# Front transfers ordered by first use, modulation weights in contiguous rows, a deeper ring of x tiles, a new simulation of transfers in the scheduler

## The chip, the cores and the metric

The kernel runs on all 8 cores of one Trainium2 chip, one batch element on each core. The metric is the device time of the slowest core in microseconds (us). A program on all cores has a second, slower state in some executions (one die at a lower clock). Engines: PE (TensorE, matmul), DVE (VectorE), ACT (ScalarE), POOL (GpSimd, which also issues the casting DMAs of weights) and SP (which issues the other DMAs).

## The reference

One decoder layer with conditioning. In outline:

```python
mod = silu(c) @ w_ada + b_ada                    # six modulation vectors of 1024; w_ada is 1024 x 6144 float32
sh1, sc1, g1, sh2, sc2, g2 = split(mod, 6)
h = rmsnorm(x, norm_mix_g) * (1 + sc1) + sh1     # x: 2048 x 1024 on each core
proj = h @ w_in                                  # 1440 columns: q and kv latents, rope key, window q, k, v
y = concat(mla_group(...), swa_group(...))       # causal latent attention, sliding-window attention
x = x + g1 * (y @ w_o)
h = rmsnorm(x, norm_mlp_g) * (1 + sc2) + sh2
x = x + g2 * (relu(h @ w_up) ** 2 @ w_down)
return rmsnorm(x, final_g)
```

## The kernel before

The tokens are worked on in four groups (0 to 3) of four x tiles (128 rows each). The "front" is what must come before steady matmul work: the first x tiles, the modulation weights (`wada`, 24 loads of 1 MB of float32, written as bf16), the input projection (`winl` for latents, `winr` for the rest), `wkvk`/`wkvv`, the rope table `csq` and the window mask `em` (1 MB).

The program lists operations with what they read and write. A list scheduler inside it simulates the engines and the DMA queues and so fixes one static order of instructions for each engine before anything runs. Each engine then works strictly in that order. The parts that matter:

```python
# --- scheduler: how long a transfer takes in its simulation (before)
if o.dma:
    free[e] = t + o.dur
    oth = "sp" if e == "pool" else "pool"
    s_ = max(chan[e], t + o.dur)
    nb = max(0.0, chan[oth] - s_) / lastpk[oth] if lastpk[oth] else 0.0
    nc_ = min(o.npk, nb)
    chan[e] = s_ + o.npk * o.pk + nc_ * lastpk[oth]
    chan[oth] += nc_ * o.pk        # but transfers already placed keep their old end
    lastpk[e] = o.pk
    o.end = chan[e] + 2000.0

# --- dependences: a later writer of a buffer waits for its earlier readers ("war")
for b in w:
    self._add_dep(op, b.w, "waw")
    for x in b.r:
        self._add_dep(op, x, "war")
# ... cut ...
NXT = 2                                              # ring of x tiles
XT, bXT = ring("XT", NXT, [128, D], F32, "SA")
# ... cut ...
# modulation weights lie over memory that attention uses later: K (rows of 256 elements,
# as K is [128, 8, 2048]) or V (contiguous)
for g in range(1, NG):
    for half in range(2):
        c0 = g * 512 + half * 256
        wada_over(f"K{g}{'ab'[half]}", a_Kg[g], K_[:, :, c0:c0 + 256])
    wada_over(f"V{g}", a_V[g], ...)                  # 4096 bytes in a row
WADA_SLOT = {4: "K1a", 5: "K1b", 6: "V1", 7: "K2a", 0: "K2b", 1: "V2", 2: "K3a", 3: "K3b", 12: "V3", 13: "K1a", 14: "K1b",
             15: "V1", 16: "K2a", 17: "K2b", 18: "V2", 19: "K3a", 8: "K3b", 9: "V3", ...}
# ... cut ...
for c in range(4):
    wada_load(4 + c)                                 # POOL queue, in this order
    win_lat(c)
for c in range(4):
    wada_load(c)
# wkvk, wkvv, winr[0], winr[1], then loads 12, 13, 14, 15, wqb, 16, ...
load_cs(0, [bWKVV])     # csq waits for wkvv to land, by being listed as a reader of it
# ... cut ...
# later: wkvv is scaled in place by DVE; as a writer of wkvv it waits for csq
S.op("dve", lambda h: h.tensor_scalar(out=WKVV[:, c, :], in0=WKVV[:, c, :], scalar1=GKVA[:, c:c + 1],
                                      scalar2=None, op0=ALU.mult), r=[bWKVV, bPAR], w=[bWKVV])
S.dma("sp", lambda h: h.dma_start(out=EM, in_=em_d), bEM, w=[bEM])
```

The softmax here doesn't subtract the row's maximum and nothing guards it: scores larger than these inputs give would overflow.

Of the kernel before, what the change touches and what calls it, by code (L numbers as in the profile page):

```python
# [86 lines left out]

class Engine:


    def __init__(self, h):
        self.h = h

    def __getattr__(self, name):
        f = getattr(self.h, name)
        return lambda *a, **k: f(*[settle_arg(x) for x in a], **{n: settle_arg(x) for n, x in k.items()})  # L96

# [29 lines left out]
class Sched:  # L127
# [115 lines left out]
    def schedule(self):  # L243
# [5 lines left out]
        for t in tenants.values():  # L249
            if t.eager:  # L250
                continue
            mine = {id(o) for o in t.ops}
            for o in t.ops[1:]:
                for (d, dv, kind) in list(o.deps):
                    if id(d) not in mine and any(set(u.allowed) & set(t.allowed) for u in d.tens):
                        t.ops[0].deps.append((d, 0, "order"))
# [12 lines left out]
        free = {e: 0.0 for e in self.ENGS}  # L269
        chan = {"pool": 0.0, "sp": 0.0}  # L270
        lastpk = {"pool": 0.0, "sp": 0.0}
        order = {e: [] for e in self.ENGS}
# [21 lines left out]
        def place(o, t):  # L294
# [27 lines left out]
            return t  # L322

        last_in = [None] * 8
        for o in self.all:
# [3 lines left out]
        while left:  # L329
            best = None  # L330
            for e in self.ENGS:
                if now[e]:
                    t = free[e]
                elif fut[e]:
                    t = max(free[e], fut[e][0][0])
                else:
                    continue
                if best is None or t < best[0]:
                    best = (t, e)
            if best is None:  # L340
                raise RuntimeError(f"no bank for {[(o.idx, o.fn.__code__.co_firstlineno) for o in parked]}")
# [15 lines left out]
            if o.dma:  # L357

                free[e] = t + o.dur
                oth = "sp" if e == "pool" else "pool"  # L360
                s_ = max(chan[e], t + o.dur)
                nb = max(0.0, chan[oth] - s_) / lastpk[oth] if lastpk[oth] else 0.0
                nc_ = min(o.npk, nb)
                chan[e] = s_ + o.npk * o.pk + nc_ * lastpk[oth]
                chan[oth] += nc_ * o.pk
                lastpk[e] = o.pk
                o.end = chan[e] + 2000.0
            else:
                o.end = t + o.dur + (165.0 if e == "pe" else 0.0)
                free[e] = max(t + 20.0, o.end - self.OVER[e] ) if e != "pe" else t + o.dur  # L370
            order[e].append(o)
            left -= 1
            for tn in o.tens:
                tn.left -= 1
                if tn.left == 0:
# [4 lines left out]
                    for w in back:  # L380
                        heapq.heappush(fut[w.eng], (max(w.rdy, min(bank_at[tn.i:tn.i + tn.width])), w.pri, w.idx))
            for j in succ[i_]:
                npred[j] -= 1
                if npred[j] == 0:
                    release(self.all[j])
        self.ops = order
        self.makespan = max(o.end for o in self.all)

    def emit(self, nc, es, block, handles):
        def newsem(name):  # L390
            return es.enter_context(nc.semaphore(name))
# [29 lines left out]
        def run(e, h):  # L421
            seen = {}
            hh = Engine(h)
            for o in self.ops[e]:
                need = {}
                for (d, dv, kind) in o.deps:
                    if skip(o, d, kind):
                        continue
                    if d.dma:
                        k, v = d.dbuf.dsem, dv  # L430
                    else:
                        k, v = esem[d.eng], d.cnt
                    kk = k.num
                    if seen.get(kk, 0) >= v:
                        continue
                    if kk not in need or need[kk][1] < v:
                        need[kk] = (k, v)
                for kk, (k, v) in need.items():
                    h.wait_ge(k, v)  # L439
                    seen[kk] = v  # L440
                ins = o.fn(hh)
                if o.dma:
                    ins.then_inc(o.dbuf.dsem, 16)
                elif o.sig:
                    ins.then_inc(esem[e], 1)
# [79 lines left out]
def build_program():  # L525
# [29 lines left out]
    with es:  # L555
# [9 lines left out]
        def bk(t, rows=None, cols=None):  # L565
            r0, r1 = rows if rows else (0, 128)
            c0, c1 = cols if cols else (0, 512)
            return Lazy(lambda: PS[r0:r1, t.i or 0, c0:c1])

        def bk_bf(t):  # L570
            return Lazy(lambda: PS[:, t.i or 0, :].bitcast(BF16))

        def bk_pair(t):
            return Lazy(lambda: PS[:, t.i or 0:(t.i or 0) + 2, :])

# [143 lines left out]

        for g in range(1, NG):  # L720
            for half in range(2):
                c0 = g * 512 + half * 256
                wada_over(f"K{g}{'ab'[half]}", a_Kg[g], K_[:, :, c0:c0 + 256])
            wada_over(f"V{g}", a_V[g], AR.ap(Alloc("", a_V[g].lo, a_V[g].lo + 4096, ""), [128, 8, 256], BF16))
        for i in range(4):
            WADA[f"B{i}"], bWADA[f"B{i}"] = one(f"WADAB{i}", [128, 8, 256], BF16, "B")
        WADA_SLOT = {4: "K1a", 5: "K1b", 6: "V1", 7: "K2a", 0: "K2b", 1: "V2", 2: "K3a", 3: "K3b", 12: "V3", 13: "K1a", 14: "K1b",
                     15: "V1", 16: "K2a", 17: "K2b", 18: "V2", 19: "K3a", 8: "K3b", 9: "V3", 10: "V3", 11: "V3",
                     20: "B0", 21: "B1", 22: "B2", 23: "B3"}
# [61 lines left out]
        def load_x(t, after=()):  # L791
            s_ = t % NXT
            S.dma("sp", lambda h: h.dma_start(out=XT[s_], in_=x_d[t * 128:(t + 1) * 128, :]), bXT[s_], r=after,
                  w=[bXT[s_]])

        for t in range(NXT):
            load_x(t)
# [78 lines left out]
        def a_norm(G):  # L876
            st = nxt_of("sta", 4)
            for j in range(4):
                t = 4 * G + j
                if t >= NXT:  # L880
                    load_x(t, [[], [bWINL[2]], [bWINR[0]], [bWINR[1]]][G])
                sumsq(XT[t % NXT], bXT[t % NXT], st, j, XN[t % 4], bXN[t % 4])
                rstd4(st, j, 1, D)
                S.op("dve", lambda h, t=t, j=j: h.tensor_scalar(out=XN[t % 4], in0=XT[t % NXT], scalar1=STA[st][:, 8 + j:9 + j],
                                                               scalar2=None, op0=ALU.mult),
                     r=[bXT[t % NXT], bSTA[st]], w=[bXN[t % 4]])

# [188 lines left out]
        S.dma("pool", lambda h: h.dma_start(out=WQB.rearrange("p a b -> p (a b)"), in_=wqb_d), bWQB, w=[bWQB])  # L1076
        for n2 in (16, 17, 18, 19, 8):
            wada_load(n2)
# [18 lines left out]
        for n2 in (12, 13, 14, 15):  # L1097
            ada_step(n2)
        wada_load(9)
        a_rope(1)  # L1100
# [37 lines left out]
        SWA_SCALE = 0.125  # L1138
        S.dma("sp", lambda h: h.dma_start(out=EM, in_=em_d), bEM, w=[bEM])

# [10 lines left out]
        def score(t):  # L1151
            return Lazy(lambda: PS.rearrange("p a b -> p (a b)")[:, 512 * (t.i or 0):512 * ((t.i or 0) + t.width)])

# [521 lines left out]
```

## Time and profile before

| | before |
|---|---|
| time, 40 runs: median (lowest) | 913.6 us (910.8) |
| profiled run, slowest core | 912.8 us |
| PE busy | 807.3 us, 88% |
| 512 B weight packets in the first 130 us (packet records) | 12288 |
| wkvv lands / csq of group 0 lands | 60.2 / 73.8 us |

The page of the kernel before: busy time, then the span in 40 slices of 22.8 us (tenths of busy time; PEclk is the granted PE clock; DMA is the mean busy share of 16 engines), then DMA packets by size.

```profile
span 912.8 us, 15934 instructions; the slowest of 8 cores (897.4 to 912.8 us)
...
PE 807.3 (88%) x5578; PEld 408.2 (45%) x5578; DVE 390.8 (43%) x677; ACT 408.6 (45%) x662; POOL 199.2 (22%) x164
...
PE   0536989989989897867989999999999999999996
...
PEclk9967899999999999979989999999999999999999
DMA  9999972164032548967482004140223511002113
...
DMA packets 47469, 101.47 MB, mean 111 GB/s; under 512 B 3488, under 2 KB 24096, under 8 KB 47264
```

In the first three slices PE is mostly idle while the DMA row is full. The sixteenth to nineteenth slice (342 to 433 us) are a second thin place: the output projection, overlapped with attention's end.

The chain of waits of the kernel before, two pieces of it (start us, length, what):

```profile
10.75 49.40 DMA arena<-wkvv
60.22 13.61 DMA arena<-csq
74.65 0.76 DVE arena L96
75.55 3.16 PE ps L96 x22
...
368.84 14.80 DMA x1s<-arena
383.76 9.13 DMA arena<-x
```

The front ends when wkvv has landed, then csq. In the second thin place the chain is a store of an x1 tile, then the load of an x tile behind it. All the kernel's own instructions carry line 96 in this trace, because of a helper.

Waits of the kernel before in the first 130 us (engine waiting, what for, us in total, times, longest):

```profile
PE ps L96 <- DMA arena<-wada: 15.5, 2, 15.0
DVE arena L96 <- DMA arena<-csq: 13.7, 1, 13.7
```

Busy time by stretches (us from the start: PE, PE loads, DVE, ACT, POOL; granted clock, DMA share, GB/s as written):

```profile
core 5: us, PE busy (x) PEld busy (x) DVE busy (x) ACT busy (x) POOL busy (x), PEclk, DMA share, GB/s
60.00:75.00 15.00, 3.17 (x9) 0.71 (x9) 1.13 (x4) 5.75 (x13) 0.00 (x0) 0.50 0.98 153
85.00:115.00 30.00, 29.79 (x255) 16.23 (x253) 15.14 (x27) 12.63 (x25) 0.76 (x1) 0.91 1.11 207
370.00:400.00 30.00, 18.66 (x159) 9.45 (x157) 8.73 (x14) 14.19 (x26) 2.29 (x2) 0.88 0.93 262
```

PE does 3.2 us of work between 60 and 75 us and is full from 85 to 115. The clock of 0.50 in the empty stretch is what the Trainium skill ("TensorE: Matmul & The Clock Gate", Part 1) describes, a half clock after an idle window of about 3.4 us. This trace agrees: its half-clock records last 3.4 us or multiples of it (the one that the end cuts off aside). At half clock PE also works at half pace: matmuls of 512 columns follow each other every 427 ns in these records and every 216 ns at full clock. So an idle gap can cost a little more than its length.

### The profile page before, as it was taken

How to read it: one execution, taken by the hardware profiler on the slowest of the kernel's cores; microseconds unless marked ns; L12 is line 12 of the kernel's file. 1: busy time of each engine (PE TensorE's matmuls, PEld its weight loads, DVE VectorE, ACT ScalarE, POOL GpSimd, SP SyncE). 2: the span in 40 equal slices, each digit the busy share in tenths (PEclk: the TensorE clock that was granted, in tenths of full speed). 3: DMA queues.
4: the chain of work that ended last, by engine and by line, in shares of the span. 5: the costliest groups of instructions: out<-in, count | busy, mean ns of one | idle time of the engine just before them, and what ended most of it. 6: DMA issues, size and time to landing. Idle time of an engine off the chain costs nothing.

```text
span 912.8 us, 15934 instructions; the slowest of 8 cores (897.4 to 912.8 us)
## 1 busy us (share of the span) xinstructions
PE 807.3 (88%) x5578; PEld 408.2 (45%) x5578; DVE 390.8 (43%) x677; ACT 408.6 (45%) x662; POOL 199.2 (22%) x164
## 2 busy tenths in 40 slices
PE   0536989989989897867989999999999999999996
PEld 0323545655546454434444444444444444444442
DVE  1325477465253448335646112441115533325546
ACT  2244376686888685535200443224442224224334
POOL 6010065265369552100034000000000000111120
PEclk9967899999999999979989999999999999999999
DMA  9999972164032548967482004140223511002113
GB/s 190 200 177 179 226 139 66 53 111 113 35 64 56 172 142 237 228 219 232 169 199 78 1 8 86 48 138 1 41 52 93 184 60 57 24 1 92 69 65 144
DMA packets 47469, 101.47 MB, mean 111 GB/s; under 512 B 3488, under 2 KB 24096, under 8 KB 47264
## 3 DMA queue, kind: packets, MB, share of 16 engines
q1 hardware_dynamic: 28432, 73.06, 25.1%
q0 software_dynamic: 18960, 27.40, 19.3%
q8 instruction: 47, 0.77, 0.3%
q14 instruction: 30, 0.25, 0.1%
HBM read 104.77 MB, written 20.97 MB: 138 GB/s over the span
## 4 chain that ended last, share of the span: by engine, by line
PE 78%; DMA 11%; ACT 3%; DVE 3%; issue 3%; POOL 2%; SPq 0%; DVEq 0%; ACTq 0%; POOLq 0%
PE ps L96 78%; DMA arena<-wkvv 5%; DVE arena L96 3%; ACT arena L96 3%; POOL arena L96 2%; DMA x1s<-arena 2%; DMA arena<-csq 1%; DMA arena<-wdn 1%; DMA arena<-x 1%; DMA mxs<-arena 1%; ACT ps L96 0%; SPq L96 0%; DVEq L439 0%; ACTq L439 0%; SPq L439 0%
## 5 line engine op out<-in xcount | busy, mean ns | idle before, releaser
L96 PE MATMUL ps<-arena 128*128 128x512 bf16 (+4 forms) x5578 | 807.3, 305 | 96.5 <-DVE arena L96 63.6
L96 PEld LDWEIGHTS ps<-arena 128*128 128x128 bf16 x5578 | 408.2, 99 | 495.1 <-issue 162.3
L96 ACT ACTIVATE arena<-ps 128x1024 bf16<-128x1024 f32 (+4 forms) x319 | 243.9, 787 | 330.7 <-PE ps L96 328.0
L96 DVE TENSOR_TENSOR arena<-ps,arena 128x512 f32<-128x512 f32 (+5 forms) x292 | 152.2, 535 | 257.4 <-PE ps L96 243.8
L96 POOL TENSOR_TENSOR arena<-arena 128x512 bf16<-128x512 bf16 (+3 forms) x103 | 162.8, 1593 | 420.7 <-DVE arena L96 246.7
L96 ACT ACTIVATE arena<-arena 128x512 bf16<-128x512 f32 (+3 forms) x264 | 149.0, 570 | 153.8 <-DVE arena L96 74.3
L96 DVE TENSOR_TENSOR arena<-arena 128x1024 bf16<-128x1024 f32 (+4 forms) x51 | 63.8, 1255 | 31.8 <-DMA arena<-wdn 28.9
L96 DVE COPY arena<-ps 128x512 f32<-128x512 f32 (+2 forms) x64 | 41.2, 656 | 71.6 <-PE ps L96 65.4
L96 DVE TENSOR_SCALAR arena<-arena 128x1024 bf16<-128x1024 f32 (+3 forms) x40 | 30.1, 754 | 54.6 <-ACT arena L96 38.0
L96 POOL DMA_DIRECT2D arena<-wup x16 | 8.7, 555 | 175.5 <-PE ps L96 175.5
L96 DVE TENSOR_SCALAR arena<-ps,arena 128x512 bf16<-128x512 bf16 (+1 forms) x72 | 34.9, 533 | 18.1 <-PE ps L96 17.7
L96 DVE TENSOR_SCALAR arena<-ps 128x512 f32<-128x512 f32 x32 | 21.7, 688 | 43.3 <-PE ps L96 39.2
L96 POOL DMA_DIRECT2D arena<-wada x24 | 18.7, 782 | 77.8 <-PE ps L96 76.1
L96 DVE SCALAR_TENSOR_TENSOR arena<-arena 128x1024 f32<-128x1024 f32 (+1 forms) x23 | 21.3, 926 | 9.7 <-ACT arena L96 9.1
L96 DVE SCALAR_TENSOR_TENSOR arena<-arena,ps 128x512 bf16<-128x512 f32 x20 | 13.7, 741 | 4.0 <-ACT ps L96 2.7
L96 ACT ACTIVATE arena<-ps,arena 128x512 bf16<-128x512 f32 x12 | 8.3, 688 | 12.0 <-PE ps L96 12.0
L96 DVE RECIPROCAL arena<-ps 128x4 f32<-128x4 f32 x32 | 5.6, 176 | 17.5 <-PE ps L96 17.4
L96 DVE CAST arena<-ps 128x512 bf16<-128x512 f32 x16 | 10.4, 687 | 2.2 <-PE ps L96 2.2
L96 ACT ACTIVATION_READ_ACCUMULATOR arena<-arena 128x1 f32 x49 | 9.2, 189 | 0.0
L96 ACT ACTIVATE ps<-ps,arena 128x512 f32<-128x512 f32 x8 | 5.2, 662 | 0.8 <-PE ps L96 0.8
L96 POOL DMA_DIRECT2D arena<-wo x8 | 4.4, 559 | 4.7 <-PE ps L96 4.7
L96 ACT ACTIVATE ps<-ps 128x512 f32<-128x512 f32 x8 | 4.5, 595 | 0.2
(14 smaller groups left out, 16.0 us busy)
## 6 DMA issues: line engine op xcount, KB each, us to landing
arena<-x SPq DMA_DIRECT2D x32, 512.0 KB, 8.0
arena<-wdn SPq DMA_DIRECT2D x32, 512.0 KB, 4.1
arena<-wada POOLq DMA_DIRECT2D x24, 512.0 KB, 37.3
arena<-wup POOLq DMA_DIRECT2D x16, 512.0 KB, 10.0
out<-arena SPq DMA_DIRECT2D x15, 512.0 KB, 2.6
x1s<-arena SPq DMA_DIRECT2D x12, 512.0 KB, 5.2
arena<-x1s SPq DMA_DIRECT2D x12, 512.0 KB, 3.2
mxs<-arena SPq DMA_DIRECT2D x12, 256.0 KB, 3.6
```

Of the source, the lines that this page charges most:

```text
L96: return lambda *a, **k: f(*[settle_arg(x) for x in a], **{n: settle_arg(x) for n, x in k.items()})
```

## The change

The intent is to bring bytes in the order in which they are first needed, in longer rows, with more x tiles under way. Five parts, cut to their core (the scheduler deals out eight banks, parts of the memory that matmuls write to):

```diff
@@ memory: slots of the modulation weights
-        for g in range(1, NG):
+        for g in (2, 3):
             for half in range(2):
                 wada_over(f"K{g}{'ab'[half]}", ...)      # rows of 256 elements
+        # contiguous slots of 4096 B over V, window q, mix, PE32, em and QG buffers
-        WADA_SLOT = {4: "K1a", 5: "K1b", 6: "V1", 7: "K2a", 0: "K2b", 1: "V2", 2: "K3a", 3: "K3b", 12: "V3", 13: "K1a", 14: "K1b",
-                     15: "V1", 16: "K2a", 17: "K2b", 18: "V2", 19: "K3a", 8: "K3b", 9: "V3", ...
+        WADA_SLOT = {4: "V1", 5: "V2", 6: "V3", 7: "SWQ0", 0: "SWQ1", 1: "PE32", 2: "EM", 3: "MIX0", 12: "MIX1", 13: "QG", 14: "V1",
+                     15: "PE32", 16: "V2", 17: "V3", 18: "K2a", 9: "K2b", 19: "K3a", 8: "K3b", ...
@@ x tiles: five slots for groups 0 and 1, four loads at once
+        XTS = [0, 1, 2, 3, 0, 1, 4, 3] + [0, 1] * 4
-        for t in range(NXT):
+        for t in range(4):
             load_x(t)
@@ em after w_in, load 9 earlier
-        S.dma("sp", lambda h: h.dma_start(out=EM, in_=em_d), bEM, w=[bEM])
+        S.dma("sp", lambda h: h.dma_start(out=EM, in_=em_d), bEM, r=[bWINR[1]], w=[bEM])
@@ scheduler: the simulation of transfers
-                chan[e] = s_ + o.npk * o.pk + nc_ * lastpk[oth]
-                chan[oth] += nc_ * o.pk
-                o.end = chan[e] + 2000.0
+                dma_run(t)                     # both queues advance together, a packet of each in turn;
+                queue[e].append([o, o.npk])    # a transfer ends only when its packets have gone
@@ scheduler: banks
-                    if id(d) not in mine and any(set(u.allowed) & set(t.allowed) for u in d.tens):
+                    if id(d) not in mine and d.tens and (d.eng == "pe" or any(set(u.allowed) & set(t.allowed) for u in d.tens)):
```

The rest of the diff makes the program build faster and gives instructions their own line numbers. It does not touch csq's false reader.

More of the change, by code (lines that the diff above doesn't have):

```diff
@@ L86, in settle_arg, with lazy, settle_views @@
     return v.get() if type(v) is Lazy else v
-class Engine:
-    def __init__(self, h):
-        self.h = h
-    def __getattr__(self, name):
-        f = getattr(self.h, name)
-        return lambda *a, **k: f(*[settle_arg(x) for x in a], **{n: settle_arg(x) for n, x in k.items()})
+EMITTING = [False]
+def lazy(fn):
+    return fn() if EMITTING[0] else Lazy(fn)
+def settle_views(f):
+    for c in f.__closure__ or ():
+        if type(c.cell_contents) is Lazy:
+            c.cell_contents = c.cell_contents.get()
+    if f.__defaults__:
+        f.__defaults__ = tuple(settle_arg(v) for v in f.__defaults__)
 class Op:
@@ L269, in schedule @@
         free = {e: 0.0 for e in self.ENGS}
-        chan = {"pool": 0.0, "sp": 0.0}
-        lastpk = {"pool": 0.0, "sp": 0.0}
+        queue = {"pool": [], "sp": []}
+        dma_t = [0.0]
         order = {e: [] for e in self.ENGS}
@@ L322, in place, with dma_next, dma_run, done @@
             return t
+        def dma_next():
+            a, b = queue["pool"], queue["sp"]
+            if a and b:
+                n = min(a[0][1], b[0][1])
+                return dma_t[0] + n * (a[0][0].pk + b[0][0].pk), n
+            if a or b:
+                q = (a or b)[0]
+                return dma_t[0] + q[1] * q[0].pk, q[1]
+            return None
+        def dma_run(to):
+            a, b = queue["pool"], queue["sp"]
+            if to > dma_t[0] and (a or b):
+                n = (to - dma_t[0]) / sum(q[0][0].pk for q in (a, b) if q)
+                for q in (a, b):
+                    if q:
+                        q[0][1] -= n
+            dma_t[0] = max(dma_t[0], to)
+        def done(o):
+            for j in succ[o.idx]:
+                npred[j] -= 1
+                if npred[j] == 0:
+                    release(self.all[j])
         last_in = [None] * 8
@@ L339, in schedule @@
                     best = (t, e)
+            nd = dma_next()
+            if nd is not None and (best is None or nd[0] <= best[0]):
+                dma_run(nd[0])
+                for q in queue.values():
+                    if q and q[0][1] <= 1e-6:
+                        d = q.pop(0)[0]
+                        d.end = nd[0] + 2000.0
+                        done(d)
+                continue
             if best is None:
@@ L359, in schedule @@
                 free[e] = t + o.dur
-                oth = "sp" if e == "pool" else "pool"
-                s_ = max(chan[e], t + o.dur)
-                nb = max(0.0, chan[oth] - s_) / lastpk[oth] if lastpk[oth] else 0.0
-                nc_ = min(o.npk, nb)
-                chan[e] = s_ + o.npk * o.pk + nc_ * lastpk[oth]
-                chan[oth] += nc_ * o.pk
-                lastpk[e] = o.pk
-                o.end = chan[e] + 2000.0
+                dma_run(t)
+                queue[e].append([o, o.npk])
             else:
@@ L381, in schedule @@
                         heapq.heappush(fut[w.eng], (max(w.rdy, min(bank_at[tn.i:tn.i + tn.width])), w.pri, w.idx))
-            for j in succ[i_]:
-                npred[j] -= 1
-                if npred[j] == 0:
-                    release(self.all[j])
+            if not o.dma:
+                done(o)
         self.ops = order
@@ L389, in emit @@
     def emit(self, nc, es, block, handles):
+        EMITTING[0] = True
         def newsem(name):
@@ L422, in run @@
             seen = {}
-            hh = Engine(h)
             for o in self.ops[e]:
@@ L440, in run @@
                     seen[kk] = v
-                ins = o.fn(hh)
+                settle_views(o.fn)
+                ins = o.fn(h)
                 if o.dma:
@@ L567, in bk @@
             c0, c1 = cols if cols else (0, 512)
-            return Lazy(lambda: PS[r0:r1, t.i or 0, c0:c1])
+            return lazy(lambda: PS[r0:r1, t.i or 0, c0:c1])
         def bk_bf(t):
-            return Lazy(lambda: PS[:, t.i or 0, :].bitcast(BF16))
+            return lazy(lambda: PS[:, t.i or 0, :].bitcast(BF16))
         def bk_pair(t):
-            return Lazy(lambda: PS[:, t.i or 0:(t.i or 0) + 2, :])
+            return lazy(lambda: PS[:, t.i or 0:(t.i or 0) + 2, :])
         def take_bank(allowed, width=1):
@@ L718, in wada_over, with over, wada_one @@
             bWADA[name] = Buf(a2.name, a2)
-        for g in range(1, NG):
+        def over(name, bases, nbytes):
+            a2 = Alloc(name, bases[0].lo, bases[0].lo + nbytes, "SA")
+            assert all(b.lo == a.hi for a, b in zip(bases, bases[1:])) and bases[-1].hi >= a2.hi
+            for b in bases:
+                a2.overl.append(b)
+                b.overl.append(a2)
+            return a2
+        def wada_one(name, bases):
+            a2 = over("WADA" + name, bases, 4096)
+            WADA[name], bWADA[name] = AR.ap(a2, [128, 8, 256], BF16), Buf(a2.name, a2)
+        for g in (2, 3):
             for half in range(2):
@@ L723, in build_program @@
                 wada_over(f"K{g}{'ab'[half]}", a_Kg[g], K_[:, :, c0:c0 + 256])
-            wada_over(f"V{g}", a_V[g], AR.ap(Alloc("", a_V[g].lo, a_V[g].lo + 4096, ""), [128, 8, 256], BF16))
+        for g in range(1, NG):
+            wada_one(f"V{g}", [a_V[g]])
+        for i in range(2):
+            wada_one(f"SWQ{i}", [bSWQ_[i].alloc])
+            wada_one(f"MIX{i}", [bMIX[2 * i].alloc, bMIX[2 * i + 1].alloc])
+        wada_one("PE32", [bPE32[0].alloc])
+        wada_one("EM", [bEM.alloc])
+        wada_one("QG", [b.alloc for b in bQG[0:4]])
+        xt_over = [over("XT2", [bH1T[1][0].alloc], 4096), over("XT3", [b.alloc for b in bPT[0:2]], 4096),
+                   over("XT4", [b.alloc for b in bPTS[0:2]], 4096)]
+        for a2 in xt_over:
+            XT.append(AR.ap(a2, [128, D], F32))
+            bXT.append(Buf(a2.name, a2))
+        XTS = [0, 1, 2, 3, 0, 1, 4, 3] + [0, 1] * 4
         for i in range(4):
             WADA[f"B{i}"], bWADA[f"B{i}"] = one(f"WADAB{i}", [128, 8, 256], BF16, "B")
-        WADA_SLOT = {4: "K1a", 5: "K1b", 6: "V1", 7: "K2a", 0: "K2b", 1: "V2", 2: "K3a", 3: "K3b", 12: "V3", 13: "K1a", 14: "K1b",
-                     15: "V1", 16: "K2a", 17: "K2b", 18: "V2", 19: "K3a", 8: "K3b", 9: "V3", 10: "V3", 11: "V3",
+        WADA_SLOT = {4: "V1", 5: "V2", 6: "V3", 7: "SWQ0", 0: "SWQ1", 1: "PE32", 2: "EM", 3: "MIX0", 12: "MIX1", 13: "QG", 14: "V1",
+                     15: "PE32", 16: "V2", 17: "V3", 18: "K2a", 9: "K2b", 19: "K3a", 8: "K3b", 10: "V3", 11: "V3",
                      20: "B0", 21: "B1", 22: "B2", 23: "B3"}
@@ L791, in load_x @@
         def load_x(t, after=()):
-            s_ = t % NXT
+            s_ = XTS[t]
             S.dma("sp", lambda h: h.dma_start(out=XT[s_], in_=x_d[t * 128:(t + 1) * 128, :]), bXT[s_], r=after,
                   w=[bXT[s_]])
-        for t in range(NXT):
+        for t in range(4):
             load_x(t)
@@ L879, in a_norm @@
                 t = 4 * G + j
-                if t >= NXT:
+                if t >= 4:
                     load_x(t, [[], [bWINL[2]], [bWINR[0]], [bWINR[1]]][G])
-                sumsq(XT[t % NXT], bXT[t % NXT], st, j, XN[t % 4], bXN[t % 4])
+                sumsq(XT[XTS[t]], bXT[XTS[t]], st, j, XN[t % 4], bXN[t % 4])
                 rstd4(st, j, 1, D)
-                S.op("dve", lambda h, t=t, j=j: h.tensor_scalar(out=XN[t % 4], in0=XT[t % NXT], scalar1=STA[st][:, 8 + j:9 + j],
+                S.op("dve", lambda h, t=t, j=j: h.tensor_scalar(out=XN[t % 4], in0=XT[XTS[t]], scalar1=STA[st][:, 8 + j:9 + j],
                                                                scalar2=None, op0=ALU.mult),
-                     r=[bXT[t % NXT], bSTA[st]], w=[bXN[t % 4]])
+                     r=[bXT[XTS[t]], bSTA[st]], w=[bXN[t % 4]])
         def a_tr(G, kp):
@@ L1076, in build_program @@
         S.dma("pool", lambda h: h.dma_start(out=WQB.rearrange("p a b -> p (a b)"), in_=wqb_d), bWQB, w=[bWQB])
-        for n2 in (16, 17, 18, 19, 8):
+        for n2 in (16, 17, 18, 9, 19, 8):
             wada_load(n2)
@@ L1098, in build_program @@
             ada_step(n2)
-        wada_load(9)
         a_rope(1)
@@ L1151, in score @@
         def score(t):
-            return Lazy(lambda: PS.rearrange("p a b -> p (a b)")[:, 512 * (t.i or 0):512 * ((t.i or 0) + t.width)])
+            return lazy(lambda: PS.rearrange("p a b -> p (a b)")[:, 512 * (t.i or 0):512 * ((t.i or 0) + t.width)])
         class MlaUnit:
```

## The prediction

> **What bounds the kernel now.** TensorE is busy for 88% of the span (the page), but not in the front. By stretches, PE works 23.5 us of the first 75, 8.5 of 75–85, 29.8 of 85–115, 17.3 of 115–135, then over 90%. The DMA engines are busy all through 5–130 us (the page's DMA row). Counting float32 source bytes (weights are cast to bf16 on the way), about 17.5 MB arrive by 60 us, some 300 GB/s. The Trainium skill ("HBM Reference", Specifications) gives 358 GB/s per core when both of a pair stream; the trace runs at about 85% of that. So the front is limited by bytes and their order.
>
> The chain of waits: wkvv landing from 10.8 to 60.2 us, then the csq table until 73.8 (13.6 us for 256 KB, sharing the engines with w_in's 6.6 KB packets of 0.7–0.8 us), then DVE, then PE at 75.5. VectorE stands 13.7 us on csq because csq is issued after wkvv as its "reader", and scaling wkvv must wait for that reader. Behind it stands the normalization of x tile 7, so the group-1 transposes wait too.
>
> **What the change does.**
> 1. em (1 MB) moves from 2.4 us to after w_in: 1.05/0.3 = 3.5 us less DMA ahead of wkvv.
> 2. Twelve modulation loads had 1024 packets of 512 B (mean 67 ns: 4.3 us of 16 engines each); now most have 128 of 4 KB (324–400 ns: 2.6–3.2 us). But elapsed throughput differs less: stretches of nearly only 512 B packets move 300–310 source GB/s, those with 4 KB packets 320–330. Six such loads ahead of wkvv save perhaps 1–3 us, not 7.
> 3. Four x tiles go out at once; x2, x3 were issued at 17 us or later, x6, x7 up to 49 us. Latents of group 0 can run near 33 us instead of 42–47, and group 1's transposes (3.8 us of PE, 3.4 of DVE) can fill the wait for wkvv.
> 4. Some weight slots no longer wait for an earlier load's use. The scheduler's DMA model also changes, so instructions elsewhere are reordered; an uncosted shift of a few us either way.
>
> **Critical path.** wkvv lands near 54–56 us instead of 60. csq behind it still takes 10–13 us: nothing removes that false wait. VectorE goes on at about 67–69; PE's steady run starts 5–7 us earlier with up to 4 us of transposes done: 5–11 us in all. Some is given back, because bytes up to 130 us are the same: em, bada, csq and x8–x11 now crowd 65–90 us, and wqb (landed 94.1, DVE waited 2.1 us) may come only 4 us earlier, a longer wait there. After 135 us PE should merely shift.
>
> Prediction 904 us, 8 in 10 between 892 and 912. Faster by over 2% (below 895): 0.17; within 2%: 0.81; slower: 0.02.
>
> **What would show it.** (a) em lands after w_in; (b) packets of 512 B in the first 130 us fall from 12288 to about a third; (c) wkvv lands near 55; (d) VectorE still waits 8–13 us on csq; (e) group-0 latents by 37 us, group-1 transposes before csq; (f) PE's dense run starts near 66–70 rather than 75.5; (g) PE busy stays near 807 us; (h) PE idle outside the front unchanged within 4 us.
>
> **What would make it wrong.** Throughput of 4 KB rows far above 330 GB/s, or the new order freeing DVE from csq: 890–895. A new DVE stall on wqb, or PE on late modulation weights: 910 or more. Or the reordering changes attention and the output stage (DMA waits of 5–15 us near 300, 370–392 and 422 us).

## The result

| | before | after |
|---|---|---|
| median (lowest) | 913.6 us (910.8), 40 runs | 902.3 us (899.3), 20 runs |
| ratio of fast runs | | 0.9889, 95% interval 0.9874 to 0.9904 |
| PE busy, profiled core | 807.3 us | 808.4 us |
| 512 B weight packets in the first 130 us | 12288 | 4096 |
| wkvv / csq land | 60.2 / 73.8 us | 54.8 / 67.6 us |

A ratio here is the mean time of one kernel's fast runs over that of the other's in the same rounds, so it is not quite the ratio of the quoted medians.

The page of the kernel after, the lines that answer to those of before:

```profile
span 902.4 us, 15926 instructions; the slowest of 8 cores (887.2 to 902.4 us)
...
PE 808.4 (90%) x5578; PEld 409.4 (45%) x5578; DVE 387.9 (43%) x677; ACT 407.3 (45%) x662; POOL 198.9 (22%) x164
...
PE   0659699999999897898788999999999999999996
...
PEclk9959799999999997999899999999999999999998
DMA  9999952075042549968471022220313411002113
...
DMA packets 40301, 101.47 MB, mean 112 GB/s; under 512 B 3488, under 2 KB 15904, under 8 KB 40096
```

The bytes are the same, the packets 7168 fewer. PE is fuller in the second to fourth slice and thinner in the fifth (90 to 113 us). Next, the chain of waits of the kernel after:

```profile
8.53 46.28 DMA arena<-wkvv
54.88 12.70 DMA arena<-csq
...
67.95 0.75 DVE arena L1004
68.84 1.69 PE ps L842 x7
...
365.64 11.55 DMA x1s<-arena
377.32 4.34 DMA arena<-x
```

wkvv lands 5.4 us earlier and csq still follows it. The waits of the kernel after in its first 130 us:

```profile
PE ps L842 <- DMA arena<-wada: 17.9, 2, 11.2
...
DVE arena L1096 <- DMA arena<-csq: 2.6, 1, 2.6
```

DVE now waits 2.6 us for csq instead of 13.7: the order puts the norms and the evacuation of group 1's transposes ahead of scaling wkvv. The stretches of the kernel after:

```profile
core 0: us, PE busy (x) PEld busy (x) DVE busy (x) ACT busy (x) POOL busy (x), PEclk, DMA share, GB/s
60.00:75.00 15.00, 11.54 (x46) 4.20 (x47) 8.10 (x15) 10.78 (x18) 0.00 (x0) 0.85 1.00 203
85.00:115.00 30.00, 21.05 (x166) 12.19 (x165) 15.94 (x32) 9.76 (x22) 0.00 (x0) 0.83 1.16 237
370.00:400.00 30.00, 25.75 (x242) 14.49 (x240) 12.54 (x26) 18.00 (x28) 2.30 (x2) 0.94 0.83 267
```

There are three movements: more PE work early, less between 85 and 115 us, more between 370 and 400 us. The bare windows mix them, because the two kernels are at different points of their work. So the rest of this text uses **milestones: the time at which PE has done 25, 40, 60 ... us of its work, taken from the trace's matmul records of one profiled run, mean of the eight cores**. The standard deviation between cores is 1 to 3.4 us at 60 us of work and 2 to 9 us late, so the mean of eight is known to about 1 us early and 1 to 3 late. Differences in microseconds from before are in brackets.

| PE work done, us | 25 | 40 | 60 | 100 | 300 | 330 | 430 |
|---|---|---|---|---|---|---|---|
| before | 76.3 | 92.2 | 112.4 | 156.3 | 371.1 | 412.1 | 522.2 |
| after | 63.7 (-12.6) | 80.0 (-12.2) | 104.2 (-8.2) | 148.2 (-8.1) | 365.7 (-5.4) | 400.9 (-11.3) | 512.0 (-10.2) |

The front gains 12.6 us. By 60 us of work 4.4 are given back, and by 300 another 2.8 (no more than its error). The output stage (300 to 330) then gains 5.9.

A caution, which the comparisons below need: PE time at half clock is counted here like any other, though it does half the work, so a kernel whose front runs at a lower clock reaches an early milestone too soon. The trace's clock records allow a correction, each microsecond of PE work weighted with the granted clock; a table of it stands under e10. The correction leaves most of after's gain (11.2 us at 25), but not that of some of the runs below.

What happens there shows in the chain's two DMA pieces above: together 23.9 us in before and 15.9 in after. The SP queue's timelines, before and then after (start us, length, what):

```profile
381.54 0.61 SPq L96 DMA_DIRECT2D arena<-h2s  x1
...
383.76 8.43 SPq L96 DMA_DIRECT2D arena<-x  x3
```

```profile
377.32 0.33 SPq L1381 DMA_DIRECT2D arena<-x  x1
...
378.91 0.87 SPq L1453 DMA_DIRECT2D arena<-h2s  x1
```

Before, the x tile that the chain needs was issued behind a 1 MB load of h2, which only the MLP needs; after, ahead of it. PE's timeline of before, and the chain's stretch in before and in after:

```profile
393.82 0.59 PE L96 MATMUL ps<-arena 128*128 128x512 bf16 x1 [7.60 <-DVE arena L96]
...
368.84:392.89 24.05, 15.93 (x146) 8.50 (x143) 7.40 (x12) 13.25 (x23) 2.29 (x2) 0.93 1.01 272
```

```profile
365.64:381.66 16.02, 14.63 (x140) 8.19 (x138) 6.79 (x11) 12.30 (x22) 2.09 (x2) 1.00 0.96 278
```

PE stood 7.6 us at the end of that chain in before and was busy for 15.9 of its 24.0 us. In after it is busy for 14.6 of 16.0 us and goes on soon after. No line of the change's data parts touches these transfers: the scheduler's order does. That the place of the h2 load alone is the reason was not isolated.

### The profile page after: what moved, and what is told of

Same layout as the page of the kernel before. It is cut to its first block, busy times and chain, and to the rows that moved or that the text cites. A ratio compares the mean times of both kernels' runs of the same rounds, so it can differ in the third digit from the quotient of the medians.

```text
span 902.4 us, 15926 instructions; the slowest of 8 cores (887.2 to 902.4 us)
## 1 busy us (share of the span) xinstructions
PE 808.4 (90%) x5578; PEld 409.4 (45%) x5578; DVE 387.9 (43%) x677; ACT 407.3 (45%) x662; POOL 198.9 (22%) x164
## 4 chain that ended last, share of the span: by engine, by line
PE 76%; DMA 16%; DVE 3%; ACT 2%; issue 2%; POOL 1%; SPq 0%; DVEq 0%; ACTq 0%; POOLq 0%
PE ps L842 63%; PE ps L1225 6%; DMA arena<-wkvv 5%; DMA arena<-wdn 3%; PE ps L1249 3%; DMA arena<-arena 2%; DMA arena<-csq 1%; DMA x1s<-arena 1%; PE ps L1272 1%; DMA arena<-h2s 1%; PE ps L1297 1%; PE ps L1334 1%; DMA mxs<-arena 1%; PE ps L1414 1%; DVE arena L1449 1%
## 5 line engine op out<-in xcount | busy, mean ns | idle before, releaser
L842 PE MATMUL ps<-arena 128*128 128x512 bf16 (+3 forms) x3380 | 684.7, 353 | 37.2 <-DMA arena<-wada 17.9
L1476 ACT ACTIVATE arena<-ps 128x512 f32<-128x512 f32 x96 | 57.3, 597 | 261.4 <-PE ps L842 261.3
L1233 ACT ACTIVATE arena<-ps 128x1024 bf16<-128x1024 f32 (+1 forms) x160 | 138.3, 896 | 56.5 <-PE ps L1249 35.3
L1614 DVE TENSOR_TENSOR arena<-ps,arena 128x512 f32<-128x512 f32 x104 | 70.8, 689 | 148.7 <-PE ps L842 148.1
L928 ACT ACTIVATE arena<-arena 128x1024 bf16<-128x1024 f32 x47 | 49.6, 1056 | 117.4 <-DVE arena L1614 35.6
L1225 PE MATMUL ps<-arena 128*128 128x512 bf16 (+3 forms) x416 | 88.6, 309 | 4.2 <-ACT arena L1233 3.0
L1279 POOL TENSOR_TENSOR arena<-arena 128x1024 bf16<-128x1024 f32 x31 | 74.4, 2399 | 42.2 <-PE ps L1249 17.6
L1238 POOL TENSOR_TENSOR arena<-arena 128x512 bf16<-128x512 bf16 x32 | 39.2, 1226 | 153.0 <-ACT arena L1233 152.8
L1249 PE MATMUL ps<-arena 128*128 128x65 bf16 x1088 | 65.4, 195 | 2.6 <-ACT arena L1233 1.1
L1478 ACT ACTIVATE arena<-arena 128x512 bf16<-128x512 f32 x96 | 60.4, 629 | 8.7
L1449 DVE TENSOR_TENSOR arena<-arena 128x1024 bf16<-128x1024 f32 x32 | 41.6, 1306 | 37.6 <-DMA arena<-wdn 37.5
L1388 DVE TENSOR_TENSOR arena<-ps,arena 128x512 f32<-128x512 f32 x32 | 22.0, 686 | 26.3 <-PE ps L842 16.2
## 6 DMA issues: line engine op xcount, KB each, us to landing
arena<-x SPq DMA_DIRECT2D x32, 512.0 KB, 9.5
arena<-wdn SPq DMA_DIRECT2D x32, 512.0 KB, 4.3
arena<-wada POOLq DMA_DIRECT2D x24, 512.0 KB, 38.6
arena<-wup POOLq DMA_DIRECT2D x16, 512.0 KB, 9.5
out<-arena SPq DMA_DIRECT2D x15, 512.0 KB, 2.6
x1s<-arena SPq DMA_DIRECT2D x12, 512.0 KB, 5.8
arena<-x1s SPq DMA_DIRECT2D x12, 512.0 KB, 3.2
```

Of the source, the lines that this page charges most:

```text
L842: S.op("pe", lambda h, i=i: h.matmul(out, lhsT=lhs_list[i], rhs=rhs_list[i], start=(i == 0), stop=(i == n - 1)), r=rbufs[i], w=[bankb[bank]])
L928: S.op("act", lambda h: h.activation(out=dst, in_=src, func=AF.Square, accum_out=STA[st][:, j:j + 1]), r=[bsrc], w=[bSTA[st], bdst])
L1225: S.op("pe", lambda h, c=c, j=j, q0=q0, n=n: h.matmul(score(t)[:, c:c + n], lhsT=K_[:, hh, j * 128:(j + 1) * 128], rhs=QG[q][:, q0:q0 + n] ...
L1233: S.op("act", lambda h: h.activation(out=PT[p][:, 0:n], in_=score(t)[:, 0:n], func=AF.Exp, scale=MLA_SCALE), r=[t.buf], w=[bPT[p]])
L1238: S.op("pool", lambda h: h.tensor_tensor(out=v, in0=v, in1=TRI.unsqueeze(1).to_broadcast([128, m, 128]), op=ALU.mult), r=[bPT[p], bTRI], w ...
L1249: sp=(self.last and i == len(blocks) - 1): h.matmul(bk(ob, None, (qb * 65, qb * 65 + 65)), lhsT=PT[p][:, c:c + 128], rhs=vaug(j, hh), star ...
```

## The experiments

Theory F: the front gains from its data (fewer bytes ahead of wkvv, longer rows, more x tiles at once). Theory O: the order of instructions, from a better simulation of transfers, makes the gain. All ratios are of fast runs, against the kernel before in the same rounds; a time in us beside them is the median of all runs, slow ones included. The kernel after was measured at 0.9889 in its own rounds.

### 1. Two by two: data and order

**e1**: the kernel before with the scheduler's new function, nothing else.

```diff
-    def schedule(self):  # of before
+    def schedule(self):  # of after
```

> The kernel before with only the scheduler's new transfer model and bank rule, no buffer, slot or em change. Theory F (the front gains because fewer bytes and longer rows come ahead of wkvv and more x tiles go out at once): the landing of wkvv stays near 60 us, the PE milestones of the front (time at which 25 us of PE work are done, mean of the eight cores: 76.3 before, 63.7 after) stay within 3 us of before, and the time is 910 to 915. Theory O (the new order of instructions makes the gain): the milestone falls by more than 6 us and the time is 902 to 907.

Measured: 909.1 us, ratio 0.9933 (0.9916 to 0.9951). Milestones: 25 at 67.6 (-8.8), 60 at 106.0 (-6.3), 300 at 368.4 (-2.6), 330 at 403.8 (-8.4). wkvv landed at 61.5. So F alone is wrong: with every byte where it was, the order is worth 6 us, a little less than O expected.

The new function holds two changes, the simulation of transfers and the rule for banks, and no run separates them. The orders themselves can be compared without a chip: built with the bank rule alone, the kernel before keeps its order on every engine up to PE's 666th matmul (126 to 135 us in the trace of before). So what the order does in the front comes from the simulation. Further on both move instructions, and how the rest divides is not shown.

**e2**: the kernel after with the scheduling function of before.

```diff
-    def schedule(self):  # of after
+    def schedule(self):  # of before
```

> The kernel after with the scheduling function of before (old transfer model and bank rule), all data changes kept. F: wkvv lands at 54 to 56 us, the 25 us milestone stays within 3 us of after's 63.7, time 901 to 906. O: the milestone goes back by more than 6 us, time 909 to 915. The part of the gain that comes after 300 us of PE work (5.5 us in the profiles) should vanish under both if it is only reordering.

Measured: ratio 1.0071 (1.0051 to 1.0091), slower than before; the median of 932.1 us counts three slow runs, the three fast ones are 919.9 to 922.3. Its 25 us milestone, at 63.5 (-12.8), is as early as after's, but here the caution applies: counted at the granted clock e2 gains 6.2 us there against after's 11.2, and e1 5.9. So in the front, data and order bring about half each. What e2 gains is lost right after: its milestones are -9.7 at 40 and -0.4 at 100. The gain between 300 and 330 is absent, as expected under both theories. Neither theory foresaw that the data changes alone would cost time. Two lines of its trace show one reason, from the timelines of POOL and of PE (start us, length, what, [idle before, and what ended it]):

```profile
44.46 0.53 POOL L839 DMA_DIRECT2D arena<-wada  x1 [15.77 <-PE ps L815]
...
124.15 0.57 PE L815 MATMUL ps<-arena 128*128 128x1 bf16 x16 [5.41 <-DMA arena<-wada]
```

A modulation load was issued last of all, at 44.5 us, since its slot (PE32) was in use until then, and PE stood for it at 124 us. By the slot table that is load 15, and the next run tests it.

**e10**: e2 with a slot of its own for load 15, free from the start.

```diff
+        wada_one("MTS", [b.alloc for b in bMTS])
-                     15: "PE32", 16: "V2", ...
+                     15: "MTS", 16: "V2", ...
```

> Kernel e2 (all data changes, old transfer model; 1.007 of before) with modulation load 15 in a slot of its own that is free from the start, instead of one that waits for load 1's use. In e2's trace it is the last to be issued (44.5 us) and PE stands 5.4 us at 124 us for it. Theory: a slow e2 comes from the order that the old model builds, which asks for weights before they can have landed: with load 15 early, that wait goes, the 100 us milestone of PE work comes 4 to 6 us earlier than e2's 156.0 and the ratio falls to 0.999 to 1.003. Rival: the wait is only replaced by the next one in the same stretch (ScalarE and VectorE chains into group 1's attention), milestone within 2 us of e2's and ratio 1.004 to 1.009.

Measured: ratio 0.9988 (0.9964 to 1.0012), 7.6 us better than e2. The 100 us milestone moved from 156.0 to 149.3, and no wait of PE for a modulation weight is left between 60 and 165 us. So load 15's slot explains e2's loss against before. The gain of 4.6 us that e10 keeps at the 430 milestone shows as only 1 us in the time, because it comes from the measure. PE's busy time is 807.5 us in e10 and 807.8 in e2 against 803.1 in before (means of eight cores), but weighted with the granted clock it is 785.4, 784.4 and 785.4: the same work, more of it at a lower clock. The milestones so weighted:

| PE work at the granted clock, us | 25 | 60 | 100 | 430 |
|---|---|---|---|---|
| before | 81.8 | 121.6 | 163.3 | 539.9 |
| after | 70.6 (-11.2) | 115.9 (-5.7) | 157.3 (-6.0) | 529.8 (-10.1) |
| e1 | 75.9 (-5.9) | 119.3 (-2.3) | 161.6 (-1.7) | 534.7 (-5.2) |
| e2 | 75.6 (-6.2) | 125.3 (+3.7) | 170.2 (+6.9) | 546.8 (+6.9) |
| e10 | 75.6 (-6.2) | 119.0 (-2.6) | 160.8 (-2.5) | 539.7 (-0.2) |
| e5 (part 2) | 74.1 (-7.7) | 118.7 (-2.9) | 159.7 (-3.6) | 533.5 (-6.4) |

The last column agrees with the measured times to about 3 us, its own error. Counting the columns of the matmuls instead of their time gives the same picture of the front (-12.6 for after, -7.9 for e1, -6.5 for e2 and -6.2 for e10 at the same share of the work).

| fast-run ratio | order by the old model | order by the new model |
|---|---|---|
| data of before | 1 | 0.9933 |
| data of after | 1.0071 | 0.9889 |
| data of after, load 15 free | 0.9988 | not run |

In the front the parts nearly add; in the time they do not. The order is worth 6 us on the old data and 16 to 17 us on the new. The new data gains 4 us with the new order and loses 6.5 us with the old.

### 2. The data, part by part

**e3**: em without its new wait.

```diff
-        S.dma("sp", ..., bEM, r=[bWINR[1]], w=[bEM])
+        S.dma("sp", ..., bEM, w=[bEM])
```

> The kernel after with em issued at once as before (1 MB ahead of wkvv). F: wkvv lands 3 to 4 us later (58 us), the 25 us milestone is 2 to 4 us later, time 904 to 907. Rival: the move only shifts the collision, since em lands at 94 us in after and x tiles 10 and 11 stand behind it in its queue (x10 lands at 96, and PE idles 8 us of 97 to 105): then the 60 us milestone comes no later, and the time is 899 to 903.

Measured: 904.3 us, ratio 0.9888. But em was issued at 53.6 us, not at once: modulation load 2 lies in em's buffer and had to be used first. The run did not put em ahead of wkvv, so it does not test F's point. It does show that em landing at 67 us instead of 94 changes nothing (60 us milestone 104.9).

**e7**: em truly ahead, load 2 elsewhere.

```diff
-        wada_one("EM", [bEM.alloc])
+        wada_one("MTS", [b.alloc for b in bMTS])
-                     2: "EM",
+                     2: "MTS",
+        # and em as in e3
```

> The kernel after with em truly ahead: issued at once, with modulation load 2 put into the slot of the mix transposes instead of em's (in run e3 that slot held em back until 53.6 us, so e3 did not test the order of bytes). My step 1: wkvv lands 3.5 us later (58 us), 25 us milestone 2 to 4 us later than 63.7, time 904 to 906. Rival: as many us are won back behind, where em no longer stands with x tiles 10 and 11, time within 1.5 us of after's.

Measured: em issued at 4.0 us; wkvv landed at 59.1 (4.3 us later than in after; on the mean of the eight cores 58.5 against 55.7, 2.8 later); 25 us at 66.5 (2.8 later). Then 60 us at 104.9 (0.7 later), and a ratio of 0.9888 (0.9864 to 0.9912), after's own. So em's megabyte moves the landing about as the prediction had it (3.5), and all of it is won back by 60 us of work: the rival is right.

**e5**: rows alone. The same slots and, on every engine, the same instructions in the same order as after (the two orders were compared and differ in nothing but the transfers' shape). Each contiguous load is written backwards in 8 pieces, so that no two pieces join.

```diff
-  h.dma_start(out=WADA[s_], in_=wada_d[n2]...)
+  h.dma_start(out=turn(WADA[s_]), in_=turn(wada_d[n2]...))   # turn: pieces of 256 elements, stride -256
+  # the scheduler still counts one row of 2048, so the order stays
```

> The kernel after, instruction for instruction in the same order and with the same slots, but the modulation weights that it loads in rows of 2048 elements go down in 8 pieces of 256 (written backwards on both sides, so that no two join): 1024 packets of 512 B for each load instead of 128 of 4 KB. My prediction: the eight loads ahead of wkvv cost 1 to 3 us more, wkvv lands at 56 to 58 us instead of 55, the 25 us milestone of PE work is 1 to 3 us later than 63.7, time 903 to 905. Rival, if the summed packet time decides (4.3 us of 16 engines against 2.6 to 3.2): wkvv 9 us later, time above 908. Second rival: short rows cost nothing in elapsed time, wkvv within 0.7 us and time as after's.

Measured: 909.1 us, ratio 0.9958 (0.9936 to 0.9981), which is 6 us worse than after (e7 and e9, in the same rounds, reached 0.9888 and 0.9876). wkvv landed at 57.7, 2.9 us later, as predicted (58.3 on the mean of eight cores, 2.6 later). The tile view of wkvv, in after and then in e5 (issue length, time of issue; then time to landing):

```profile
L880 POOL DMA_DIRECT2D arena<-wkvv x1: 638/638/638, 8.5 to 8.5; - x1
...
DMA to landing us min/median/max: 46.3/46.3/46.3
```

```profile
L880 POOL DMA_DIRECT2D arena<-wkvv x1: 659/659/659, 11.4 to 11.4; - x1
...
DMA to landing us min/median/max: 46.3/46.3/46.3
```

POOL needs a median of 0.96 us for each modulation load of 1024 packets against 0.62 over all of after's, and the first weight packet leaves at 6.4 us against 4.4 (packet records). Between 15 and 50 us the queues moved 309 GB/s of source bytes (a casting transfer counted at twice what it wrote) against 331. That the pieces run backwards is not what costs: their packets took 68 ns in the mean against 67 for those of before, which run forwards.

The milestones hardly move (-1.5 at 25, +1.4 at 40, +0.9 at 430), but at the granted clock e5 is 3.5 us behind after at 25 and 3.7 at 430 (table above). Since the order is the same, single matmuls can be compared too. On the six cores whose traces hold all 5578 in both runs, e5's 300th ends 4.8 us later than after's (which ends at 71 us), the 1000th (159 us) 3.5 us and the last 5.7 us later, with errors of 0.6, 1.3 and 3.4. So the loss arises in the front and stays. DVE's wait for csq is part of it: 5.6 to 6.6 us on the eight cores of e5, 0.3 to 3.2 in after. The rows are worth more than the 1 to 3 us predicted.

**e6**: two x slots.

```diff
-        XTS = [0, 1, 2, 3, 0, 1, 4, 3] + [0, 1] * 4
+        XTS = [0, 1] * 8
-        for t in range(4):            # and "if t >= 4" below
+        for t in range(2):            # and "if t >= 2"
```

> The kernel after with two slots for the x tiles instead of five, rescheduled by its own model. If the deeper ring matters in the front (my step 3): x tiles 2 and 3 are issued later, group 0's latents come later (the 10 us milestone from 35.3 to 38 or more), group 1's transposes no longer all fit before csq, the 25 us milestone 3 us or more later than 63.7, time 904 to 908. Rival: kernel before with the new model alone reached 33.7 and 67.6 at these milestones with two slots, so the ring is worth at most 4 us at 25 us and the time is 901 to 904.

Measured: 904.3 us, ratio 0.9908 (0.9885 to 0.9931). The 10 us milestone is at 39.0 (35.3 in after), 25 us at 67.4 (+3.7; +1.9 at the granted clock), 60 at 106.2 (+2.0), 330 at 401.7 (+0.8). The ring does what step 3 said in the front, and about 2 us or less of it reaches the end, inside the interval.

### 3. The false wait for csq

**e9**: after in exactly its order, with only that wait taken off (csq does not touch wkvv, so nothing races).

```diff
+        cs0 = load_cs(0, [bWKVV])
         S.schedule()
+        for o in S.all:
+            if o.eng == "dve":
+                o.deps = [d for d in o.deps if not (d[0] is cs0 and d[2] == "war")]
         S.emit(nc, es, block, None)
```

> The kernel after in exactly its order, with the false wait alone taken away: scaling wkvv no longer waits for the csq transfer, which touches other memory (no race). In the trace of after VectorE waited 2.6 us there, and PE 2.5 us behind it. If that is its whole cost, the 25 us milestone comes 2 to 3 us earlier, and the time is 899 to 902. If the wait of 8 to 13 us that I predicted were hidden in it, 892 to 896. Rival: nothing left at the 60 us milestone, because the x tiles of group 2 and the order of ScalarE set the pace there, time within 1 us of after's.

Measured: 902.4 us, ratio 0.9876 (0.9847 to 0.9905). 25 us at 63.4 (-0.3 from after), 60 at 104.7 (+0.5). Matmul by matmul, as for e5, e9 is 1.3 to 2.1 us ahead of after between 71 and 97 us (error 0.7 to 0.9), and 0.5 to 1.8 us later on, inside the error. So the wait costs 1 to 2 us in the front, about what the trace shows, and the ratio leaves room for about 1 us at the end, which is not told from zero.

**e4**: csq issued when the last latent columns have landed, order free.

```diff
-        load_cs(0, [bWKVV])
+        load_cs(0, [bWINL[3]])
```

> The kernel after with csq of group 0 issued when the last piece of w_in's latent columns has landed (about 33 us), so that the scaling of wkvv no longer waits for it. My prediction called this false wait 8 to 13 us long; the trace of after shows VectorE waiting only 2.6 us for it. If it costs what the trace shows: time 898 to 901 and the 25 us milestone 2 to 4 us earlier. If it were worth 8 to 13: 890 to 895. Rival: nothing, 901 to 904, because the x tiles behind em set the pace 30 us later anyway.

Measured: csq issued at 33.3 us; 907.0 us, ratio 0.9922 (0.9889 to 0.9955), no better than after and probably worse. 25 us at 64.5, 60 at 106.2. The scheduler answered the earlier table with another order, so this run mixes the wait with the order; e9 is the clean one.

### 4. How much does an order move by chance?

**e8** and **e12**: after with one constant of the simulation nudged.

```diff
-                        d.end = nd[0] + 2000.0
+                        d.end = nd[0] + 2300.0        # e8
-    LAT = {"pe": 146.0, ...
+    LAT = {"pe": 156.0, ...                           # e12
```

> A control: the kernel after, with one constant of its transfer model changed (2.3 us instead of 2.0 from the last packet to the landing), so that only the static order of instructions changes. It measures how much a reordering without any aim moves the time. If the order is tuned only in its large features: within 2 us of after's 902.3. If a reordering by chance is worth as much as the effects of em, ring and csq that I measured (0 to 4 us): 899 to 908, and those effects are then not told from it.

> A second control: the kernel after with 156 instead of 146 ns assumed for a semaphore to reach the matmul engine. Same reading: within 2 us of after if only large features of the order matter, up to 6 us away if chance reordering matters.

Measured: e8 905.0 us, ratio 0.9903 (0.9864 to 0.9943); e12 905.6 us, ratio 0.9923 (0.9891 to 0.9956). The 25 us milestone stays (63.3 and 63.8), 330 is at 398.5 and 400.3. So an aimless reordering moved the time by up to 3 us in two tries. The net effects of em, ring and csq, and e4's loss, are no larger than that. The front's gain and the order's 6 and 16 us are, and so is the output stage's gain: between 300 and 330 all eleven kernels ordered by the new function (e5 and e9 share after's order) gain 5.4 to 8.0 us over before, and e2 and e10, with the old one, lose 0.8 and 0.6.

### 5. A version that follows from this: em later still

In after, x tile 10 stands behind em in the SP queue: em is issued at 69.4 us and takes 25.0 to land. ACT's and PE's timelines of the kernel after:

```profile
96.24 1.06 ACT L928 ACTIVATE arena<-arena 128x1024 bf16<-128x1024 f32 x1 [2.93 <-DMA arena<-x]
...
99.45 0.27 PE L955 MATMUL ps<-arena 128*128 128x128 bf16 x1 [2.62 <-DVE arena L943]
...
104.92 0.48 PE L955 MATMUL ps<-arena 128*128 128x128 bf16 x3 [3.95 <-DVE arena L1015]
```

ACT waits for the tile, then PE waits twice for the norms and scalings behind it. **e11** holds em until modulation load 18 has landed.

```diff
-        S.dma("sp", ..., bEM, r=[bWINR[1]], w=[bEM])
+        S.dma("sp", ..., bEM, r=[bWADA['K2a']], w=[bEM])
```

> The kernel after with em held until modulation load 18 has landed (about 95 us instead of 69 us issued), so that x tiles 10 and 11 go ahead of it. If em ahead of them caused the idle PE of 97 to 113 us in after (4 us of the front's gain given back): the 60 us milestone of PE work comes 2 to 4 us earlier than 104.2, time 898 to 901. Rival, from e3 and e7 where em had landed long before and the milestone stayed at 104.9: the chain of norms on ScalarE and VectorE and its place in the static order hold PE there, milestone within 1.5 us, time 901 to 905.

Measured: em issued at 101.5 us; 899.7 us, ratio 0.9861 (0.9829 to 0.9893). 60 us of work at 101.9 (2.3 earlier than after), 100 at 146.2 (2.0 earlier), 300 at 361.0 (4.7 earlier). It beats before. Against after it is 2.6 us better, with overlapping intervals and a size no larger than an aimless reordering. The stage moved as expected, and both controls left that stage where it was or 0.9 us later; but e3 and e7, where em was out of the way too, had no gain there. (At the granted clock e11 is 5.9 us earlier than after at 60, the controls 2.3 and 1.3, e3 and e7 1.1 and 2.7, so the reading is the same.) So em ahead of the tiles is not shown to be the cause: the place of those norms in the new static order may be.

## Why the prediction was right or wrong

The total was right: 904 us predicted, 902.3 measured, inside 892 to 912. The sum got there with terms that were off in both directions, which is luck in part: the prediction looked for the gain in the front alone, but of the front's 12.6 us only 5.4 are left by 300 us of work, and the output stage, to which it gave nothing, brings another 5.9.

- **The front is limited by bytes and their order: right, with one limit.** By the packet records 17.0 MB of source arrived by 54.8 us in after and 17.9 MB by 60.2 in before; em is the difference. The rate of 331 GB/s between 15 and 50 us is 92% of the share that the Trainium skill names ("HBM Reference", Specifications). The limit: e1 brought the 25 us milestone 8.8 us forward (5.9 at the granted clock) with those bytes unchanged, so the order makes about half of the front's gain.
- **wkvv near 55: right** (54.8). Its two terms measured alone, on the mean of eight cores: em 2.8 us (predicted 3.5), short rows 2.6 us (1 to 3); their sum, 5.4, is close to the 4.9 us by which wkvv came earlier in after (60.6 to 55.7).
- **csq behind wkvv takes 10 to 13 us: right** (12.7). The Trainium skill ("DMA: Bandwidth & Descriptors", Queues, rings and completion order) says that a DMA engine goes round robin among queues, packet by packet. The trace agrees: csq's 128 packets of 2 KB, 8 for each engine if they are spread evenly, took 0.16 us each in the mean but started over 7.3 us (58.6 to 65.9), about one in 0.9 us; a packet of csq and one of w_in's 6.6 KB (0.67 in the mean) together take 0.83.
- **"VectorE still waits 8–13 us on csq": this step failed.** It waited 2.6 us (0.3 to 3.2 on the eight cores, 8.4 to 14.4 in before), since other work now stood ahead of the scaling of wkvv, and e9 shows that these 2.6 us cost 1 to 2 in the front and 1 at most in the time. I read the old trace's wait as a property of the dependence. It was a property of the dependence and of the work that the order puts ahead of it. Either half of the change shortens it: the waits of e1 (new order, old data) and of e2 (old order, new data):

```profile
DVE arena L96 <- DMA arena<-csq: 4.3, 1, 4.3
```

```profile
DVE arena L1069 <- DMA arena<-csq: 5.2, 1, 5.2
```

- **"PE's steady run starts 5–7 us earlier with up to 4 us of transposes done: 5–11 us in all": too small for the front.** The dense run began at 68.8 us instead of 75.5 as predicted and group 1's transposes ran before csq, but by 25 us of PE work the gain was 12.6. Counted at the granted clock it was 11.2, the top of the range.
- **"Some is given back": right, 4.4 us by 60 us of work, with the wrong cause.** DVE does not wait for wqb in after (it landed at 91.8). The gap is the chain of norms of x tiles 10 and 11 and its place in the order; which of the two is open (e3, e7, e11).
- **"The scheduler's DMA model also changes ...; an uncosted shift of a few us either way" and "After 135 us PE should merely shift": these failed.** The scheduler's function alone was worth 6 us, and without it the data changes lose 6.5 us (e1, e2, e10). It also gained 5.9 us in the output stage (see the result). I had put PE's idle time outside the front as unchanged within 4 us. The net from 60 us of work to 430 is 2.0, made of +2.8, -5.9 and +1.1.
- **Group 0's latents by 37 us: late.** Their matmuls ran from 30.5 to 41.5 us in after, against 33.5 to 47.2 for transposes and latents in before.
- **em after w_in, a third of the 512 B packets, PE busy unchanged: right** (em landed at 94.4, w_in at 68.2; 4096 of 12288; 808 us).

What remains open: how the order's gain after the front divides between the simulation and the bank rule, why e2 and e10 run more of PE's work at a lower clock, and the cause of the gap that e11 narrows.

## What to carry to other kernels

When a program fixes its order from a simulation, a change of data and a change of the simulation are one change: run the two by two before crediting either, because here the data changes alone made the kernel slower and a single weight slot that came free late was most of that. Read a wait in a trace together with what stands behind it in its engine's order, and take the wait alone away in the unchanged order before counting on it. Nudge a constant that should not matter to learn how much reordering by chance is worth, and do not interpret effects smaller than that (3 us here). And when the clock varies, measure progress in work done, not in busy time: here busy time made a front that gained 6 us look like one that gained 12.8.

## What the Trainium skill lacked or had wrong

- "DMA: Bandwidth & Descriptors", Specifications, gives 512 B as the least transfer for line rate. Here pieces of 512 B as written (1 KB as read, cast on the way) moved 309 GB/s of source bytes where the same loads in 4 KB rows moved 331, and the kernel was 6 us slower (e5).
- The same page, in its anatomy of a POOL-issued DMA, says that many descriptors can be emitted before their cost shows. In e5, with every load in 1024 packets, a load took a median of 0.96 us to issue, against 0.62 in after, where most have 128; and the first weight packet left 2.0 us later.
- "HBM Reference" gives about 358 GB/s for each core when both of a pair stream; two queues with packets of 2.5 to 4 KB reached 331 with eight cores loading. No disagreement, but the page has no figure for such a mix.
- No page that I used speaks of static orders fixed from a simulation; the spread of 3 us between aimless reorderings (e8, e12) has no place there yet.
